# A two-layer decoder trunk on one core: a different price for VectorE in the scheduler's model, a reordered opening, priority for the normalisations between sublayers, and one convolution tap on ScalarE

## The chip, the cores and the metric

The kernel runs on one core of a Trainium2 chip. The core has TensorE (matmuls; PE, and PEld for its weight loads), VectorE (DVE), ScalarE (ACT), GpSimd (POOL) and SyncE (SP, which here only issues transfers), 16 DMA engines, SBUF as working memory and eight PSUM banks for the results of matmuls. The metric is the time of one execution on the device, in microseconds. The median of three runs before is 1197.02 us (1197.02 to 1197.41).

## The reference, cut to what matters

Two layers (`DEPTH = 2`) over 256 tokens of width 1024, in float32. Each layer has a feed-forward half-step, a token mixer with three branches, and a second feed-forward half-step; each with an RMS norm before and one behind it:

```python
for l in range(DEPTH):
    h = rms_norm(x, ffn1_norm_pre[l])
    x = x + 0.5 * rms_norm(swiglu(h, ffn1_w_in[l], ffn1_w_out[l]), ffn1_norm_post[l])
    h = rms_norm(x, mix_norm_pre[l])
    y = token_mixer(h, mem, cos, sin, ...)
    x = x + rms_norm(y, mix_norm_post[l])
    h = rms_norm(x, ffn2_norm_pre[l])
    x = x + 0.5 * rms_norm(swiglu(h, ffn2_w_in[l], ffn2_w_out[l]), ffn2_norm_post[l])
```

Inside the mixer one branch is `y_conv = bg * short_conv(cg * u, conv_w)`, a causal convolution with three taps over 512 channels; the second is an attention over compressed, selected and neighbouring tokens (8 heads in 2 groups); the third is an attention over 256 memory tokens (4 heads of 128). Their outputs are gated, added and multiplied by `w_out`. `rope_tables(positions)` gives the sine and cosine of the positions, which the second branch uses.

## The kernel before, in words

**Tiling.** The 256 tokens are two halves of 128, the streams t = 0 and t = 1; `x[0]` and `x[1]` (128 x 1024) stay in SBUF all the time. Weights come from memory in units of 512 KB (`raw`, four buffers), issued by SP in an order written out in the code. Every unit is split for accuracy: ScalarE casts it to `whi` (L326) and VectorE subtracts to get `wlo` (L327). Activations are split the same way into `hThi` and `hTlo`. A product is then three matmuls, hi by hi, lo by hi and hi by lo. Each unit is used by both streams. TensorE's largest groups are L399 (`product`, first half of a feed-forward) and L387 to L389 (`mm3`, all other products).

**Streams and steps.** A loop at the end of the program advances the two streams step by step (`now` counts the steps). Stream 0 may be `lead` steps ahead: 2 until `RAMP`, then `LEAD`. `later(n, f)` puts a piece of work off by n steps; `settled` (at step `EARLY`) and `start_setup` (at `SETUP`) are two of these.

**What sets the order.** SP's order is that of the program text. The order of all other engines is set when the program is built, by the framework's scheduler, with a model of how long each instruction takes (`TRN2Spec`); what is wrapped in `pinned` in the first steps keeps program order. On the chip every engine runs its instructions in that fixed order, and waits where an operand isn't there.

**The opening.** VectorE clears `idle` (L198), TensorE runs matmuls on it (L203, `keep_clock`) until the first data is there. SP and ScalarE each issue one half of `x[0]` (L217) and one half of the first weight unit (L305), SP then the second unit, `x[1]` (L343) and the rest. `prenorm` turns x by transposes on TensorE (`pt`, L430), multiplies by the gain on VectorE (`hf`, L500) or, of `x[1]`, in part on ScalarE (L497), casts `hThi` (L505) and subtracts `hTlo` (L506). The positions come by a transfer of single words (L676). The setup on VectorE and GpSimd (masks, and sine and cosine in some twenty small operations, L684 to L702) follows after the first steps.

**Between sublayers.** `postnorm` takes the two PSUM banks of a sublayer's output `y`: `rstd` (a sum of squares on ScalarE, `nv` on VectorE L476, a power on GpSimd), two products with the gain (`pn`, L571), and the update of x in pieces (L577). `prenorm` then transposes x (L430) and makes `hf` (L528), `hThi` and `hTlo` (L534). During this TensorE computes the other stream's products.

**The mixer.** Its names in the profile: `QT`, `z`, `u`, `zs` (compression of keys), `phc`, `oc` (attention to the compressed tokens, L1162), `sm`, `qmT`, `pm` (memory attention), `vT`, `cT`, `convT`, `bs` (the convolution: `vT` the transposed input, `convT` its weights, `cT` the result; taps in L1257 to L1259), `br`, `gth` (gated sum, L1392), `acc` and `y` (products).

Of the kernel before, what the change touches and what calls it, by code (L numbers as in the profile page):

```python
# [22 lines left out]
TRN2Spec.DMA_START_FIXED_NS = 4000.0  # L23

F32 = mybir.dt.float32
# [32 lines left out]
AWAY, SPLIT, RETURN = 1, 11, 6  # L58
MSTEP, MWAIT = (5, 11), 3
SECOND_HALF = 1  # L60
CONV, BS, CMP, ZC, QS_0, QS_1, QM, PC, YM = 7, 4, 6, 2, 2, 6, 2, 3, 1
# [101 lines left out]
def program(tc, nc, pools, a, out, plan):  # L163
# [33 lines left out]
    idle = ttile("idle", F32R)  # L197
    nc.vector.memset(f32(idle[:, :512]), 0.0)  # L198

    def keep_clock(count):  # L200
        ps = bank("idle")
        for _ in range(count):
            pinned(nc.tensor.matmul(ps, lhsT=idle[:, :P], rhs=idle[:, :512], start=True, stop=True))  # L203

    first_steps, latest = [True], [None]

# [15 lines left out]
    ident_r = consts.tile([P, P], F32R, name="ident_r")  # L222
    mhalf = consts.tile([P, 1], F32, name="mhalf")
# [8 lines left out]
    pinned(nc.vector.tensor_copy(gT[:, 0:16], gt_ps[:, :16]))  # L232

    def other_gains():
        rest = ttile("rest")
        for i in range(3):
            nc.gpsimd.dma_start(rest[i * 16:(i + 1) * 16, 0:P], a[PRE[i + 1]].rearrange("l (k p) -> (l k) p", p=P))

        def turn():
# [93 lines left out]
    def prefetch():  # L333
        if dry:
            return
        ahead = AHEAD if now[0] > RAMP else 1
        while splits and splits[0][0][0] <= now[0] + ahead and free["w"] > 0:
            split_unit()
        if now[0] == 0 and not prologue:
            prologue.append(True)  # L340
            load(loads.pop(0), (nc.sync, nc.scalar))
            load(loads.pop(0))
            nc.sync.dma_start(x[1], a["x"][0, P:2 * P, :])  # L343
# [47 lines left out]
    def product(hT, name, l, cols):  # L391
        ps = [bank("acc") for _ in cols]
        for k in range(8):
            parts = [(0, -1, name, l, k, 1, cols[0][0], cols[0][1])]
            hi, lo = unit((name, l, cols[0][0], k), parts)
            for i, (x2, w) in enumerate(((0, hi), (1, hi), (0, lo))):
                for j, p in enumerate(ps):
                    n = cols[j][1]
                    pinned(nc.tensor.matmul(p[:, :n], lhsT=hT[x2][:, k], rhs=moving(w, j * n, n),  # L399
                                            start=(k == 0 and i == 0), stop=(k == 7 and i == 2)))  # L400
            yield 0
        return ps
# [67 lines left out]
    def rstd(halves):  # L470
# [7 lines left out]
        r = sp.tile([P, 1], F32, name="nr")  # L478
        nc.gpsimd.tensor_tensor(r, v, mhalf, op=OP.pow)
        return r  # L480
# [4 lines left out]

    rest = [None, None]

    def prenorm(t, name, l, warm=False):
        src = x[t]
        hi, lo = gtile("hThi", F32R), gtile("hTlo", F32R)  # L490
        g0 = PRE.index(name) * 16 + l * 8
# [10 lines left out]

        def halved(half):
            sl = slice(half * 512, (half + 1) * 512)
            pinned(nc.scalar.copy(hi[:, sl], hf[half][:, :512]))  # L505
            pinned(nc.vector.tensor_sub(lo[:, sl], hf[half][:, :512], f32(hi[:, sl])))  # L506

        if warm and splits:
# [4 lines left out]
            gained(0, pts[0])  # L513
            split_unit(lambda: halved(0))
            split_unit()
            gained(1, pts[1])
            halved(1)
        elif rest[t] is None:
# [4 lines left out]
        else:  # L523
            pts = [transpose4(src, c, 2) for c in (0, 256)]

# [9 lines left out]

            piece(0, 2, pts[0])
            rest[t]()
            piece(256, 2, pts[1])
            parts(0, 2)
            parts(256, 2)  # L540
            rest[t] = None

            def second():
                piece(512, 4, transpose4(src, 512))
                parts(512, 4)

# [19 lines left out]
    def postnorm(y, t, key, factor, last=False):  # L566
        g = gain(*key)
        r = rstd(y)
        tmp = [ttile(f"pn{i}") for i in range(2)]
        for i in range(2):  # L570
            nc.vector.scalar_tensor_tensor(straight(tmp[i], 0, 512, 256), turned(y[i], 0, 512, 256), 32.0 * factor,  # L571
                                           straight(g, i * 512, 512, 256), op0=OP.mult, op1=OP.mult)
        drop("g", key)
# [8 lines left out]
        if last:  # L582
            for i in range(2):
                update(i, 0, 512)
        else:
            for c in (0, 256):
                update(0, c, 256)
            rest[t] = lambda: update(1, 0, 512)
# [66 lines left out]
    def setup():  # L655
# [18 lines left out]

        posi = consts.tile([P, 2], I32, name="posi")
        nc.gpsimd.dma_start(posi, a["positions"].rearrange("o (t p) -> p (o t)", p=P))  # L676
        posf = consts.tile([P, 2], F32, name="posf")
        nc.vector.tensor_copy(posf, posi)
        freq = consts.tile([P, 8], F32, name="freq")
# [43 lines left out]
    def start_setup():  # L723
        with tc.issue_after(latest[0].ins):
            setup()
# [510 lines left out]
    def conv_part(t, l, u_s, c_ps, r):  # L1236
# [5 lines left out]
        def turn():  # L1242
# [11 lines left out]
            for c in range(4):  # L1254
                dst = cT[:, c * P:(c + 1) * P]
                w = [convT[:, base + 4 * i + c:base + 4 * i + c + 1] for i in range(3)]
                nc.vector.tensor_scalar(dst, vT[:, c, 2:130], w[2], None, op0=OP.mult)  # L1257
                nc.vector.scalar_tensor_tensor(dst, vT[:, c, 1:129], w[1], dst, op0=OP.mult, op1=OP.add)
                nc.vector.scalar_tensor_tensor(dst, vT[:, c, 0:128], w[0], dst, op0=OP.mult, op1=OP.add)  # L1259
# [161 lines left out]
    while any(live):  # L1421
# [57 lines left out]
```

## Time and profile before

| | |
|---|---|
| median of 3 runs | 1197.02 us |
| profiled execution | 1197.08 us |
| its span on the engines | 1195.4 us |
| instructions | 16,637 |
| moved by DMA | 260.64 MB, mean 218 GB/s |
| matmul groups of L399 | 3 x 640 of 128x512 |
| splits (L326, L327) | 441 each, mean 1039 and 1209 ns |

The span is the time between the first and the last instruction in the trace; the profiled execution's own time has 1.7 us beside it. A row of a timeline reads: start, duration, engine, line, operation, result <- operands, shape, count, and in brackets how long the engine had been idle and what ended that. A row of the waits: engine, tile and line that waited <- engine, tile and line waited for, then total us, times, longest. `PEld` overlaps `PE`. Matmuls are pipelined: one of 128x512 is shown with 0.38 us, and the next starts before it ends. "SPq" and "POOLq" rows are the issue of a transfer, not the transfer.

### The profile page before, as it was taken

How to read it: one execution, taken by the hardware profiler on the slowest of the kernel's cores; microseconds unless marked ns; L12 is line 12 of the kernel's file. 1: busy time of each engine (PE TensorE's matmuls, PEld its weight loads, DVE VectorE, ACT ScalarE, POOL GpSimd, SP SyncE). 2: the span in 40 equal slices, each digit the busy share in tenths (PEclk: the TensorE clock that was granted, in tenths of full speed). 3: DMA queues.
4: the chain of work that ended last, by engine and by line, in shares of the span. 5: the costliest groups of instructions: out<-in, count | busy, mean ns of one | idle time of the engine just before them, and what ended most of it. 6: DMA issues, size and time to landing. Idle time of an engine off the chain costs nothing.

```text
span 1195.4 us, 16637 instructions
## 1 busy us (share of the span) xinstructions
PE 1180.4 (99%) x5776; PEld 1030.5 (86%) x5776; DVE 897.5 (75%) x1147; ACT 753.4 (63%) x1201; POOL 184.7 (15%) x332
## 2 busy tenths in 40 slices
PE   8999999999999999999999999999999999999997
PEld 6888888888888888888888888889888888888886
DVE  7867767898998786676576677588899977766753
ACT  6756746888876565565465565469878755655541
POOL 4001301501110020011021011015012100210100
PEclk9999999999999999999999999999999999999999
DMA  7887876676677757777757778757767776677771
GB/s 243 256 255 237 272 257 184 215 236 186 206 223 226 227 182 220 220 242 227 226 183 223 221 238 264 237 143 235 230 193 212 207 232 212 188 232 215 233 229 58
DMA packets 133620, 260.64 MB, mean 218 GB/s; under 512 B 15680, under 2 KB 36832, under 8 KB 133536
## 3 DMA queue, kind: packets, MB, share of 16 engines
q1 hardware_dynamic: 123616, 234.59, 63.0%
q0 software_dynamic: 9600, 24.47, 7.4%
q8 instruction: 45, 0.74, 0.2%
q10 hardware_dynamic: 320, 0.53, 0.1%
q14 instruction: 39, 0.32, 0.1%
HBM read 235.42 MB, written 2.10 MB: 199 GB/s over the span
## 4 chain that ended last, share of the span: by engine, by line
PE 60%; DVE 6%; ACT 4%; issue 2%; DMA 1%; POOL 0%; DVEq 0%; POOLq 0%; ACTq 0%
PE acc L399 26%; PE y L389 6%; PE y L387 6%; PE y L388 6%; PE acc L387 4%; PE acc L388 4%; PE acc L389 4%; DVE wlo L327 2%; PE pt L430 1%; PE br L387 1%; PE br L388 1%; PE br L389 1%; ACT whi L326 1%; ACT p L926 1%; DVE turnlo L464 1%
## 5 line engine op out<-in xcount | busy, mean ns | idle before, releaser
L327 DVE TENSOR_TENSOR wlo<-raw,whi 128x1024 fp32r<-128x1024 f32 (+2 forms) x441 | 529.1, 1209 | 207.9 <-ACT whi L326 204.6
L326 ACT CAST whi<-raw 128x1024 fp32r<-128x1024 f32 (+2 forms) x441 | 453.1, 1039 | 272.1 <-PE acc L399 118.7
L446 POOL DMA_DIRECT2D moved<-blocks x176 | 95.8, 562 | 653.4 <-DVE blocks L440 415.4
L399 PE MATMUL acc<-whi,hThi 128*128 128x512 f32 x640 | 191.0, 381 | 1.1 <-ACT hThi L505 0.6
L399 PE MATMUL acc<-whi,hTlo 128*128 128x512 f32 x640 | 191.2, 380 | 0.0
L399 PE MATMUL acc<-wlo,hThi 128*128 128x512 f32 x640 | 190.1, 379 | 0.1
L387 PE MATMUL acc<-whi,hThi 128*128 128x512 f32 (+1 forms) x480 | 182.6, 380 | 0.1
L388 PE MATMUL acc<-wlo,hThi 128*128 128x512 f32 (+1 forms) x480 | 178.7, 373 | 0.4 <-DVE wlo L327 0.4
L389 PE MATMUL acc<-whi,hTlo 128*128 128x512 f32 (+1 forms) x480 | 178.7, 373 | 0.0
L399 PEld LDWEIGHTS acc<-whi,hThi 128*128 128x128 f32 x640 | 120.2, 189 | 18.8 <-ACT hThi L505 1.0
L399 PEld LDWEIGHTS acc<-whi,hTlo 128*128 128x128 f32 x640 | 120.6, 189 | 17.9 <-DVE hTlo L534 0.7
L399 PEld LDWEIGHTS acc<-wlo,hThi 128*128 128x128 f32 x640 | 120.9, 189 | 17.5 <-DVE wlo L327 0.5
L387 PE MATMUL y<-whi,turnhi 128*128 128x512 f32 x352 | 133.7, 380 | 0.0
L388 PE MATMUL y<-wlo,turnhi 128*128 128x512 f32 x352 | 133.6, 379 | 0.0
L389 PE MATMUL y<-whi,turnlo 128*128 128x512 f32 x352 | 133.4, 379 | 0.0
L389 PEld LDWEIGHTS acc<-whi,hTlo 128*128 128x128 f32 x480 | 90.6, 189 | 12.1 <-DVE hTlo L534 0.2
L388 PEld LDWEIGHTS acc<-wlo,hThi 128*128 128x128 f32 x480 | 90.9, 189 | 10.7 <-DVE wlo L327 0.7
L387 PEld LDWEIGHTS acc<-whi,hThi 128*128 128x128 f32 x480 | 90.9, 189 | 10.6 <-ACT yf L964 0.3
L388 PEld LDWEIGHTS y<-wlo,turnhi 128*128 128x128 f32 x352 | 66.5, 189 | 9.4
L389 PEld LDWEIGHTS y<-whi,turnlo 128*128 128x128 f32 x352 | 66.5, 189 | 9.4
L387 PEld LDWEIGHTS y<-whi,turnhi 128*128 128x128 f32 x352 | 66.5, 189 | 9.3
L463 ACT CAST turnhi<-moved 128x1024 fp32r<-128x1024 f32 (+1 forms) x42 | 42.3, 1008 | 43.2 <-DMA moved<-blocks 41.5
(302 smaller groups left out, 1460.3 us busy)
## 6 DMA issues: line engine op xcount, KB each, us to landing
raw<-in_ffn_w_in_dram SPq DMA_DIRECT2D x159, 512.0 KB, 4.7
raw<-in_w_mix_in_dram SPq DMA_DIRECT2D x96, 512.0 KB, 4.5
raw<-in_ffn_w_out_dram SPq DMA_DIRECT2D x88, 512.0 KB, 4.5
moved<-blocks POOLq DMA_DIRECT2D x144, 128.0 KB, 4.2
raw<-in_ffn_w_in_dram SPq DMA_DIRECT2D x33, 256.0 KB, 3.8
raw<-in_w_mem_kv_dram SPq DMA_DIRECT2D x16, 512.0 KB, 4.7
raw<-in_w_mix_out_dram SPq DMA_DIRECT2D x16, 512.0 KB, 4.7
raw<-in_cmp_k_w_dram SPq DMA_DIRECT2D x8, 512.0 KB, 4.5
```

Source lines behind the costliest of these rows:

```text
L326: pinned(nc.scalar.copy(hi[:, c0:c1], raw[:, c0:c1]))
L327: pinned(nc.vector.tensor_sub(lo[:, c0:c1], raw[:, c0:c1], f32(hi[:, c0:c1])))
L387: nc.tensor.matmul(ps, lhsT=xh, rhs=wh, start=start, stop=False, skip_group_check=skip)
L388: nc.tensor.matmul(ps, lhsT=xh, rhs=wl, start=False, stop=False, skip_group_check=skip)
L389: nc.tensor.matmul(ps, lhsT=xl, rhs=wh, start=False, stop=stop, skip_group_check=skip)
L399: pinned(nc.tensor.matmul(p[:, :n], lhsT=hT[x2][:, k], rhs=moving(w, j * n, n), start=(k == 0 and i == 0), stop=(k == 7 and i == 2)))
L430: pinned(nc.tensor.transpose(pt[:, j * P:(j + 1) * P], src[:, c0 + j * P:c0 + (j + 1) * P], ident))
L446: nc.gpsimd.dma_start(moved[0][:, q * f:(q + 1) * f], blocks[q * 32:(q + 1) * 32, :n].rearrange("j (p f) -> j p f", p=4))
L463: nc.scalar.copy(hv, mv)
L464: nc.vector.tensor_sub(lv, mv, f32(hv))
L926: nc.scalar.activation(dst, src, AF.Exp, bias=nm[:, i:i + 1], accum_out=sums[:, k:k + 1])
```

## The change

It has four parts.

1. `TRN2Spec.CYCLE_T` of VectorE is multiplied by 1.08, so the scheduler plans with a VectorE 8% slower than its model had it. This is a number of the model; no instruction on the chip gets longer by it. The order of all engines but SP follows from it.
2. The opening: the cleared piece of `idle` is 128 wide and read four times; both halves of `x[0]` and of the first unit are issued by SP, and `x[1]`, also in halves, goes ahead of the second unit; `ident_r` goes; the positions come as two rows of 128 words in `other_gains` and are turned by a transpose; the norm of stream 1 is begun inside that of stream 0 (`prenorm_begun`); the first steps' products finish one column block before the next; until step 6 (`ABREAST`) a stream leads by one step only; the setup is issued after the first power on GpSimd.
3. `tc.high_priority(200)` around the chain in `postnorm` and `prenorm`.
4. The first tap in the code (the current token, times its weight) is an activation on ScalarE that reads the PSUM bank `pt` in place of VectorE's operation on `vT`.

```diff
+TRN2Spec.CYCLE_T[mybir.EngineType.DVE] *= 1.08
...
-    nc.vector.memset(f32(idle[:, :512]), 0.0)
+    nc.vector.memset(f32(idle[:, :P]), 0.0)
...
-        (nc.sync, nc.scalar)[half].dma_start(x[0][:, sl], a["x"][0, 0:P, sl])
+        nc.sync.dma_start(x[0][:, sl], a["x"][0, 0:P, sl])
...
+        nc.gpsimd.dma_start(whole[0:2, 0:P], a["positions"].rearrange("o (t p) -> (o t) p", p=P))
...
+            nc.tensor.transpose(pt[:, 48:50], rows[0:2, 0:P], ident[0:2, 0:2])
+            nc.vector.tensor_copy(posf, pt[:, 48:50])
...
-            load(loads.pop(0), (nc.sync, nc.scalar))
+            load(loads.pop(0), (nc.sync, nc.sync))
+            for half in range(2):
+                sl = slice(half * 512, (half + 1) * 512)
+                nc.sync.dma_start(x[1][:, sl], a["x"][0, P:2 * P, sl])
             load(loads.pop(0))
-            nc.sync.dma_start(x[1], a["x"][0, P:2 * P, :])
...
+            passes = [(i, j) for i in range(3) for j in range(len(ps))]
+            if now[0] <= 1:
+                passes.sort(key=lambda p: p[1])
...
+    def prenorm_begun(t, name, l, between):
+        hi, lo = gtile("hThi", F32R), gtile("hTlo", F32R)
+        g0 = PRE.index(name) * 16 + l * 8
+        pt = transpose4(x[t], 0)
+        yield
+        for half in range(2):
+            hf, sl = ttile("hf"), slice(half * 512, (half + 1) * 512)
+            pt = transpose4(x[t], 512) if half else pt
+            pinned(nc.vector.tensor_tensor(view(hf, 0, [[P, 4], [1, P]]), view(pt, 0, [[P, 4], [1, P]]),
+                                           view(gT, g0 + half * 4, [[1, 4], [0, P]]), op=OP.mult))
+            if half:
+                split_unit()
+                between()
+            pinned(nc.scalar.copy(hi[:, sl], hf[:, :512]))
+            pinned(nc.vector.tensor_sub(lo[:, sl], hf[:, :512], f32(hi[:, sl])))
+            yield hi, lo
...
-            pts = [transpose4(src, c, 2) for c in (0, 256)]
+            with tc.high_priority(200):
+                pts = [transpose4(src, c, 2) for c in (0, 256)]
...
-            piece(0, 2, pts[0])
-            rest[t]()
-            piece(256, 2, pts[1])
-            parts(0, 2)
-            parts(256, 2)
+            with tc.high_priority(200):
+                piece(0, 2, pts[0])
+                rest[t]()
+                piece(256, 2, pts[1])
+                parts(0, 2)
+                parts(256, 2)
...
-        with tc.issue_after(latest[0].ins):
+        with tc.issue_after(latest[0].ins), tc.issue_after(power[0].ins):
...
-                nc.vector.tensor_scalar(dst, vT[:, c, 2:130], w[2], None, op0=OP.mult)
+                nc.scalar.activation(dst, pt[:, c * P:(c + 1) * P], AF.Copy, scale=w[2])
...
-        nc.vector.tensor_copy(ident_r, ident)
-        other_gains()
+        with tc.issue_after(power[0].ins):
+            other_gains()
...
-        lead = LEAD if now[0] > RAMP else 2
+        lead = LEAD if now[0] > RAMP else 2 if now[0] > ABREAST else 1
```

The orders below are read row by row; the lines of the changed kernel have moved down (its L441 is the L430 of before, L410 is L399, L334 is L327, L1303 and L1304 are L1258 and L1259).

TensorE at the program's start, before (`x_88` is `x[0]`, `x_89` is `x[1]`):

```order
5 L430 MATMUL pt<-ident,x_88 128x128 x4
6 L203 MATMUL idle<-idle 128x512 x2
7 L399 MATMUL acc<-whi,hThi 128x512 x2
8 L399 MATMUL acc<-whi,hTlo 128x512 x2
9 L399 MATMUL acc<-wlo,hThi 128x512 x2
10 L430 MATMUL pt<-ident,x_89 128x128 x8
11 L399 MATMUL acc<-whi,hThi 128x512 x2
```

The same place on TensorE in the changed kernel:

```order
5 L441 MATMUL pt<-ident,x_88 128x128 x4
6 L205 MATMUL idle<-idle 128x512 x2
7 L441 MATMUL pt<-ident,x_89 128x128 x4
8 L410 MATMUL acc<-whi,hThi 128x512
9 L410 MATMUL acc<-whi,hTlo 128x512
10 L410 MATMUL acc<-wlo,hThi 128x512
11 L410 MATMUL acc<-whi,hThi 128x512
12 L410 MATMUL acc<-whi,hTlo 128x512
13 L410 MATMUL acc<-wlo,hThi 128x512
14 L441 MATMUL pt<-ident,x_89 128x128 x4
```

Half of the transposes of `x[1]` moved ahead of the first product, half behind it, and the first product is done one bank after the other.

TensorE at the end of layer 0's mixer, where the first normalised pieces of `x[0]` come (near 424 us in the trace of before; `y_4250` and `y_4251` are the two banks of stream 1's output), before:

```order
1734 L389 MATMUL y_4250<-whi,mTlo 128x512
1735 L430 MATMUL pt<-ident,x_88 128x128 x2
1736 L387 MATMUL y_4251<-whi,mThi 128x512
1737 L430 MATMUL pt<-ident,x_88 128x128 x2
1738 L388 MATMUL y_4251<-wlo,mThi 128x512
1739 L389 MATMUL y_4251<-whi,mTlo 128x512
```

and in the changed kernel (`y_4252` and `y_4253` are the same banks' tiles):

```order
1743 L398 MATMUL y_4252<-whi,mTlo 128x512
1744 L396 MATMUL y_4253<-whi,mThi 128x512
1745 L441 MATMUL pt<-ident,x_88 128x128 x2
1746 L397 MATMUL y_4253<-wlo,mThi 128x512
1747 L441 MATMUL pt<-ident,x_88 128x128 x2
1748 L398 MATMUL y_4253<-whi,mTlo 128x512
```

One matmul of `y` moved ahead of each pair of transposes.

VectorE in layer 0's mixer, around the second `phc` and the first stream's taps (291 to 298 us of before), before:

```order
232 L1257 TENSOR_SCALAR cT<-vT,convT 128x128 x2
233 L1258 SCALAR_TENSOR_TENSOR cT<-vT,convT,cT 128x128 x2
234 L1259 SCALAR_TENSOR_TENSOR cT<-vT,convT,cT 128x128 x2
235 L1257 TENSOR_SCALAR cT<-vT,convT 128x128 x2
236 L1258 SCALAR_TENSOR_TENSOR cT<-vT,convT,cT 128x128 x2
237 L1259 SCALAR_TENSOR_TENSOR cT<-vT,convT,cT 128x128 x2
238 L1200 TENSOR_REDUCE nmm<-sm 128x2
239 L327 TENSOR_TENSOR wlo<-raw,whi 128x1024
240 L464 TENSOR_TENSOR turnlo<-moved,turnhi 128x1024
241 L327 TENSOR_TENSOR wlo<-raw,whi 128x1024
242 L1162 TENSOR_TENSOR phc<-pt,phc 32x512
```

and in the changed kernel:

```order
235 L1303 SCALAR_TENSOR_TENSOR cT<-vT,convT,cT 128x128 x2
236 L1304 SCALAR_TENSOR_TENSOR cT<-vT,convT,cT 128x128 x2
237 L1303 SCALAR_TENSOR_TENSOR cT<-vT,convT,cT 128x128 x2
238 L1304 SCALAR_TENSOR_TENSOR cT<-vT,convT,cT 128x128 x2
239 L1245 TENSOR_REDUCE nmm<-sm 128x2
240 L334 TENSOR_TENSOR wlo<-raw,whi 128x1024
241 L475 TENSOR_TENSOR turnlo<-moved,turnhi 128x1024
242 L1207 TENSOR_TENSOR phc<-pt,phc 32x512
```

The two pairs of TENSOR_SCALAR are gone and one split (`wlo`) stands behind `phc` instead of ahead of it. On ScalarE the second stream's taps now stand as three activations, four `pm`, a copy, and the fourth activation.

More of the change, by code (lines that the diff above doesn't have):

```diff
@@ L59 @@
 MSTEP, MWAIT = (5, 11), 3
+ABREAST = 6
 SECOND_HALF = 1
@@ L202, in keep_clock @@
         for _ in range(count):
-            pinned(nc.tensor.matmul(ps, lhsT=idle[:, :P], rhs=idle[:, :512], start=True, stop=True))
-    first_steps, latest = [True], [None]
+            pinned(nc.tensor.matmul(ps, lhsT=idle[:, :P], rhs=view(idle, 0, [[0, 4], [1, P]]), start=True, stop=True))
+    first_steps, latest, power = [True], [None], [None]
     def pinned(ins):
@@ L221, in program @@
         make_identity(nc, ident)
-    ident_r = consts.tile([P, P], F32R, name="ident_r")
     mhalf = consts.tile([P, 1], F32, name="mhalf")
@@ L232, in program @@
     pinned(nc.vector.tensor_copy(gT[:, 0:16], gt_ps[:, :16]))
+    posf = consts.tile([P, 2], F32, name="posf")
     def other_gains():
-        rest = ttile("rest")
+        rest, rows, whole = ttile("rest"), ttile("rows"), ttile("whole", I32)
+        nc.gpsimd.dma_start(whole[0:2, 0:P], a["positions"].rearrange("o (t p) -> (o t) p", p=P))
         for i in range(3):
             nc.gpsimd.dma_start(rest[i * 16:(i + 1) * 16, 0:P], a[PRE[i + 1]].rearrange("l (k p) -> (l k) p", p=P))
+        nc.gpsimd.tensor_copy(rows[0:2, 0:P], whole[0:2, 0:P])
         def turn():
@@ L395, in product @@
             hi, lo = unit((name, l, cols[0][0], k), parts)
[L396 to L400, printed above, removed]
+            passes = [(i, j) for i in range(3) for j in range(len(ps))]
+            if now[0] <= 1:
+                passes.sort(key=lambda p: p[1])
+            for i, j in passes:
+                (x2, w), n = ((0, hi), (1, hi), (0, lo))[i], cols[j][1]
+                pinned(nc.tensor.matmul(ps[j][:, :n], lhsT=hT[x2][:, k], rhs=moving(w, j * n, n),
+                                        start=(k == 0 and i == 0), stop=(k == 7 and i == 2)))
             yield 0
@@ L478, in rstd @@
         r = sp.tile([P, 1], F32, name="nr")
-        nc.gpsimd.tensor_tensor(r, v, mhalf, op=OP.pow)
+        power[0] = nc.gpsimd.tensor_tensor(r, v, mhalf, op=OP.pow)
         return r
@@ L484, in tokens_last @@
         return hi.rearrange(r, k=8), lo.rearrange(r, k=8)
-    rest = [None, None]
+    rest, opened = [None, None], []
+    def prenorm_begun(t, name, l, between):
[14 more added lines that the diff above has]
+            yield hi, lo
     def prenorm(t, name, l, warm=False):
         src = x[t]
+        if opened:
+            hi, lo = next(opened.pop())
+            scale = norm_scales(src, SCALES)
+            yield NORM_B
+            return tokens_last(hi, lo), scale
         hi, lo = gtile("hThi", F32R), gtile("hTlo", F32R)
@@ L501, in gained, with upper, lower, halved @@
                                            view(gT, g0 + half * 4, [[1, 4], [0, P]]), op=OP.mult))
-        def halved(half):
+        def upper(half):
             sl = slice(half * 512, (half + 1) * 512)
             pinned(nc.scalar.copy(hi[:, sl], hf[half][:, :512]))
+        def lower(half):
+            sl = slice(half * 512, (half + 1) * 512)
             pinned(nc.vector.tensor_sub(lo[:, sl], hf[half][:, :512], f32(hi[:, sl])))
+        def halved(half):
+            upper(half)
+            lower(half)
         if warm and splits:
@@ L513, in prenorm @@
             gained(0, pts[0])
-            split_unit(lambda: halved(0))
-            split_unit()
+            halved(0)
+            other = prenorm_begun(1, name, l, lambda: lower(1))
+            next(other)
+            split_unit(lambda: None)
             gained(1, pts[1])
-            halved(1)
+            upper(1)
+            next(other)
+            opened.append(other)
         elif rest[t] is None:
@@ L567, in postnorm @@
         g = gain(*key)
[L568 to L572, printed above, removed]
+        with tc.high_priority(200):
+            r = rstd(y)
+            tmp = [ttile(f"pn{i}") for i in range(2)]
+            for i in range(2):
+                nc.vector.scalar_tensor_tensor(straight(tmp[i], 0, 512, 256), turned(y[i], 0, 512, 256), 32.0 * factor,
+                                               straight(g, i * 512, 512, 256), op0=OP.mult, op1=OP.mult)
         drop("g", key)
@@ L585, in postnorm @@
         else:
-            for c in (0, 256):
-                update(0, c, 256)
+            with tc.high_priority(200):
+                for c in (0, 256):
+                    update(0, c, 256)
             rest[t] = lambda: update(1, 0, 512)
@@ L673, in setup @@
         nc.gpsimd.memset(zc, 0.0)
[L675 to L678, printed above, removed]
         freq = consts.tile([P, 8], F32, name="freq")
```

5 lines of the change are left out of this document (3 added, 2 removed).

## The prediction

> **What bounds the kernel now.** I read the page's first part, then TensorE's waits, then the windows, then single stretches of the timeline. First the busy time of the engines:
>
> ```profile
> PE 1180.4 (99%) x5776; PEld 1030.5 (86%) x5776; DVE 897.5 (75%) x1147; ACT 753.4 (63%) x1201; POOL 184.7 (15%) x332
> ```
>
> TensorE is busy 1180.4 of 1195.4 us, and the change takes no matmul away (it adds one small transpose). So the whole stake is TensorE's idle time, 15.0 us, and the gaps too short to be counted as idle. Where it lies, by windows (us, then busy time of PE, PEld, DVE, ACT, POOL):
>
> ```profile
> 0.00:20.00 20.00, 16.41 (x66) 12.29 (x67) 12.91 (x24) 13.50 (x25) 8.30 (x42) 1.00 0.76 240
> 200.00:280.00 80.00, 78.65 (x460) 69.81 (x459) 68.55 (x109) 69.27 (x159) 23.98 (x34) 1.00 0.65 198
> 280.00:360.00 80.00, 78.92 (x417) 69.42 (x416) 77.23 (x129) 64.87 (x136) 13.52 (x27) 1.00 0.69 213
> 360.00:420.00 60.00, 60.00 (x287) 52.38 (x286) 45.55 (x51) 33.74 (x45) 2.18 (x4) 1.00 0.71 220
> 870.00:950.00 80.00, 79.24 (x418) 69.73 (x417) 76.27 (x132) 64.33 (x140) 13.61 (x27) 1.00 0.67 204
> 1180.00:1196.00 16.00, 8.71 (x41) 7.28 (x39) 5.64 (x10) 2.75 (x8) 1.11 (x2) 0.85 0.18 66
> ```
>
> The opening has 3.59 us idle, the end 7.29 (a last normalisation that the change doesn't reorder), the two mixers' windows 1.35, 1.08 and 0.76. A window inside a steady stretch (360 to 420) has none: there VectorE and ScalarE have room, and nothing can be won. In 280 to 360 VectorE is busy 77.23 of 80 and sets the pace with TensorE. TensorE's waits name the places:
>
> ```profile
> PE idle L203 <- DVE idle L198: 1.5, 1, 1.5
> PE pt L430 <- DVE x L577: 1.2, 5, 0.3
> PE z L1066 <- DVE wlo L327: 1.0, 1, 1.0
> PE pt L430 <- DVE phc L1162: 0.9, 2, 0.6
> PE pt L430 <- DMA x<-in_x_dram: 0.8, 1, 0.8
> PE br L387 <- DVE gth L1392: 0.7, 1, 0.7
> PE acc L399 <- ACT hThi L505: 0.6, 1, 0.6
> PE acc L399 <- ACT whi L326: 0.5, 1, 0.5
> PE sm L389 <- DVE qmT L422: 0.2, 1, 0.2
> ```
>
> Three families: the opening (x by DMA, hThi, whi), the transitions between sublayers (x L577), and the mixers (z, phc, gth, qmT), where VectorE is late by what stands ahead in its queue.
>
> **The opening.** Rows of the timeline, and the GB/s row of the transfers in forty slices of 0.3 us:
>
> ```profile
> 2.43 0.59 SPq L343 DMA_DIRECT2D x<-in_x_dram  x1
> 2.82 0.89 POOL L676 DMA_DIRECT2D posi<-in_positions_dram  x1
> 6.99 0.38 PE L399 MATMUL acc<-whi,hThi 128*128 128x512 f32 x1
> 7.20 0.62 ACT L326 CAST whi<-raw 128x512 fp32r<-128x512 f32 x1 [0.53 <-DMA raw<-in_ffn_w_in_dram]
> 7.85 0.69 DVE L327 TENSOR_TENSOR wlo<-raw,whi 128x512 fp32r<-128x512 f32 x1 [0.45 <-ACT whi L326]
> 9.32 1.23 DVE L327 TENSOR_TENSOR wlo<-raw,whi 128x1024 fp32r<-128x1024 f32 x1 [0.78 <-ACT whi L326]
> 10.02 1.07 PE L430 MATMUL pt<-ident,x 128*128 128x128 f32 x8 [0.80 <-DMA x<-in_x_dram]
> 18.95 0.59 PE L399 MATMUL acc<-whi,hThi 128*128 128x512 f32 x2
> ...
> posi<-in_positions_dram POOLq DMA_DIRECT2D x1, 1.0 KB, 6.7
> ...
> GB/s 0 0 0 0 0 0 96 131 333 335 225 246 328 382 396 348 335 341 335 348 416 416 430 335 138 49 48 164 341 376 359 388 408 423 396 396 416 416 382 403
> ...
> 310.04 0.38 PE L389 MATMUL acc<-whi,hTlo 128*128 128x512 f32 x1
> 310.47 0.38 PE L388 MATMUL acc<-wlo,hThi 128*128 128x512 f32 x1
> ```
>
> The last two give TensorE's steady pitch: two matmuls in 0.43 us, 0.216 each. A step of six matmuls is then 1.30 us. From the first product (6.99) to the seventh step (18.95) pass 11.96 us; six steps are 7.78 and the eight transposes of the second half 1.07, so 3.1 us are gaps. The second token half's transposes come at 10.02, because its x was loaded behind the next weights.
>
> Now x[1] goes ahead of the next weight unit, and the two streams alternate from the start (lead 1). The first 24 slices of the GB/s row sum to 1.73 MB by 7.2 us; x[0], x[1] and the first unit are 1.5 MB, so x[1] should be there at about 6.6 to 7.2 instead of near 9.8. The dip behind it (138, 49, 48) falls at 7.2 to 8.1 us, while the single-word load of the positions is in flight (issued at 2.82, landed 6.7 later); with that load gone the next unit, 2.0 MB in all, should land at about 8, as before. I replayed the new order with the row durations: first product at 7.0, now behind four transposes of x[1]; step 0 held to 8.6 by the second half's cast and subtraction (0.62 and 0.69, over at 8.54); step 1 at 9.85, when the second stream's two halves have gone through 0.69 (gain), 0.62 (hi) and 0.69 (lo) beside them; step 2 to 12.75, then 1.30 each and 0.3 of leftovers: the seventh step at 16.95 instead of 18.95. That is **−2.0 us**. The best the rows allow is −2.6 (all 3.1 gaps but the 0.45 that the second half's subtraction forces); the worst is −0.5 (the wait of 0.8 for x[1] goes, and the next weights come 0.3 late). The smaller memset, the dropped ident_r cast and the setup moved later are VectorE and GpSimd work beside this, and cost nothing while the weights arrive at 1.3 us a unit. The setup's small operations then fall later, among splits of 1.2 us with a step's room each; I take 0 for them, 0.5 at worst, which the range holds.
>
> The Trainium skill (DMA: Bandwidth & Descriptors, "Issuing engines are not separate DMA queues") says that loads issued by several engines share the same 16 DMA engines, so that spreading them saves only issue time. By it, moving ScalarE's two loads to SyncE costs their issue alone and the order of bytes is what counts; the sum would be the same.
>
> **The transitions.** One of four alike, TensorE around the first normalised x:
>
> ```profile
> 423.91 0.38 PE L389 MATMUL y<-whi,mTlo 128*128 128x512 f32 x1
> 424.59 0.41 PE L430 MATMUL pt<-ident,x 128*128 128x128 f32 x2 [0.30 <-DVE x L577]
> 424.76 0.46 PE L387 MATMUL y<-whi,mThi 128*128 128x512 f32 x1
> ```
>
> TensorE arrives at 424.13 (423.91 and one pitch) and starts at 424.59. The other half's y matmuls (L387 to L389) are ready and can fill this. With the chain at high priority one more of them, 0.216 us, stands ahead of each pair. Four such places, about 0.22 to 0.3 each with the second stream's, give **−1.0 us**. Bounds: −0.3, if the chain's own operations come later by one split of VectorE at some of them, and −2.0, if all the 1.2 us of waits and the restart behind each go. At the first transition (layer 0, near 209) the transposes move eight matmuls up and the chain too; I count it at 0.
>
> **The convolution tap.** Sixteen VectorE operations go to ScalarE:
>
> ```profile
> L1257 DVE TENSOR_SCALAR cT<-vT,convT x16: 271/275/287, 291.3 to 894.5; 128x128 f32<-128x128 f32 x16
> ...
> L1258 DVE SCALAR_TENSOR_TENSOR cT<-vT,convT,cT x16: 337/340/346, 291.7 to 894.9; 128x128 f32<-128x128 f32 x16
> ...
> L497 ACT ACTIVATE hf<-pt,gT x4: 358/366/377, 9.2 to 10.0; 128x128 f32<-128x128 f32 x4
> ```
>
> Pipelined, a VectorE tap costs about 0.2 us, so 1.6 us a layer leave an engine that is 96% busy there; ScalarE, 81% busy (64.87 of 80), gets eight activations a layer of at most 0.37 us each, at most 2.9 us of its 15 idle. The new form isn't in the trace; its bounds are 0.2 and 0.37 us, and I take the PSUM activation of L497. The tap by itself moves no end: it pays through the waits below.
>
> The Trainium skill (VectorE: DVE Perf Modes, "Mode 2×_2P") says that an SBUF tensor_scalar can give two results a cycle in fp32, which an operation on two tensors cannot; it would have me leave just this tap on VectorE. The trace agrees in direction (275 against 340 ns), but by it the relief would only be 1.6 instead of 2.1 us a layer, and the sum stays.
>
> **The mixers.** With VectorE priced 8% dearer, the order of all engines changes in detail:
>
> ```profile
> 247.16 1.39 DVE L904 TENSOR_TENSOR QT<-pt,QT 64x512 fp32r<-64x512 f32 x2
> ...
> 250.51 0.30 PE L1066 MATMUL z<-wlo,FHL 128*32 128x256 f32 x1 [0.96 <-DVE wlo L327]
> ...
> 299.94 1.71 ACT L1210 ACTIVATE pm<-pm,rm 128x256 f32<-128x256 f32 x4 [0.55 <-DVE rm L1207]
> 301.70 0.58 ACT L983 COPY yf<-oc 64x512 f32<-64x512 f32 x1
> ...
> 305.07 1.21 DVE L327 TENSOR_TENSOR wlo<-raw,whi 128x1024 fp32r<-128x1024 f32 x1
> ```
>
> phc (0.9, two places): one split of 1.21 us fewer stands ahead of the last phc, and four taps fewer, 0.8; more than either wait. −0.9. gth (0.7): two splits instead of three lie before it: −0.7. qmT (0.2): two acc matmuls, 0.43, now stand before the waiting one: −0.2. z (1.0): six acc matmuls (1.30) come between, but both QT operations (1.39) and a small one go ahead of the split it waits for: 0. Sum **−1.8**. At best all idle time of these windows and of the same stretch in layer 1 goes, −3.9; at worst none goes, and the z wait of 1.0 doubles in both layers, +2.0.
>
> **Sum.** The profiled execution took 1197.08 us (span 1195.4 and 1.7 around it), and the median is 1197.02, so the two can stand for each other. 1197.1 − 2.0 − 1.0 − 1.8 = **1192.3 us**. The best ends together give 1188.6.
>
> **Rivals.**
> - Mixers give back what they gain. For it: VectorE is full there, and at z TensorE depends on the split directly, so a wait removed can reappear at the next split. Against it: after 280 the splits are ahead (the one at 305.07 is over at 306.28 and first read at 310.47, 4.2 us). Time: 1197.1 − 3.0 = 1194.1.
> - The opening doesn't advance: the next weights, behind x[1], land late, or the second stream's split holds step 1 to past 11. Time: with −0.5, 1193.8. With the first rival as well: 1195.6, which counts as no change.
> - The change doesn't do what it says: the orders move, but the waits only change their names, in all three families. 1196 to 1197.5.
> - Slower: VectorE is held in order behind ScalarE's taps. In layer 0's second stream the last activation stands behind four pm (1.71) and a copy (0.58) on ScalarE, and VectorE's remaining taps, and the split behind them, wait for it: up to 2.3 us. Four places, two a layer, make 9.2 at most. It decides once VectorE is held longer than the lead of its splits, 4.2 us at that row; two holds and the taps' own time could reach it. If all the gains stay at 0 and a third of the 9.2 comes through, 1200.2.
>
> **How the numbers follow.** A measurement of this kernel can tell about 0.2%, 2.4 us, from no change: faster is below 1194.6, slower above 1199.4. Forecast with its spread 0.52; mixers alone failing 0.15, opening alone failing 0.12 (both mostly below 1194.6); both, or the waits only renamed, 0.14; slower 0.07. Faster: 0.52 and 0.21 of the 0.27 give 0.73; no change 0.20; slower 0.07. The range goes from the best ends, 1188.6, to 1196.3, which takes in both single failures and half of the joint one.
>
> **What would show it.** In the profile after: the seventh step of six matmuls starting near 17 instead of 18.95, and the window 0 to 20 with PE busy about 18; no wait of pt on a DMA of x; pt on x L577 below 0.4 in total; phc and gth gone from TensorE's waits; VectorE's busy time in 280 to 360 lower by some 1.6 us, ScalarE's higher by 2 to 3. It would be wrong if the z wait grew past 1.5 us, if TensorE waited for cT, yconv or whi in 290 to 330, or if new waits on wlo appeared in the opening between 15 and 30 us, where the setup now falls.

## The result, and the profile after

The changed kernel takes 1190.56 us (median of 4 runs, 1190.01 to 1190.68) against 1197.02 (1196.75 to 1197.41). The ratio is 0.9946, with a 95% interval of 0.9934 to 0.9959. The profiled execution took 1190.01 us, with a span of 1188.3 against 1195.4.

The first part of the page of the changed kernel, busy time by engine:

```profile
PE 1177.2 (99%) x5777; PEld 1032.5 (87%) x5777; DVE 891.7 (75%) x1130; ACT 755.9 (64%) x1217; POOL 177.2 (15%) x333
```

TensorE's idle time fell from 15.0 to 11.1 us (1188.3 less 1177.2). The other 3.2 of the 7.1 us are in its busy time (1180.4 to 1177.2), in which breaks between matmuls too short to be idle are counted. Its waits in the changed kernel (total us, times, longest):

```profile
PE pt L441 <- DMA x<-in_x_dram: 1.4, 1, 1.4
PE idle L205 <- DVE idle L200: 1.1, 1, 1.1
PE z L1111 <- DVE wlo L334: 1.0, 2, 0.6
PE pt L441 <- POOL kd L905: 0.4, 1, 0.4
PE z L1109 <- DVE FHL L1100: 0.2, 1, 0.2
PE acc L397 <- DVE wlo L334: 0.2, 1, 0.2
```

The waits for the normalised x, for phc, for gth and for qmT are gone. The wait for `x[1]` in the opening is longer than before (1.4 against 0.8), and the mixer of layer 0 has waits at z, kd and FHL that before had only in part. The windows of the changed kernel:

```profile
0.00:20.00 20.00, 17.43 (x76) 13.81 (x77) 12.20 (x18) 14.04 (x25) 5.90 (x26) 1.00 0.76 257
200.00:280.00 80.00, 78.20 (x456) 69.01 (x455) 67.61 (x105) 67.42 (x155) 23.68 (x34) 1.00 0.66 201
280.00:360.00 80.00, 80.00 (x422) 70.98 (x422) 76.50 (x125) 69.22 (x152) 13.51 (x27) 1.00 0.69 209
870.00:950.00 80.00, 80.00 (x421) 70.94 (x420) 77.36 (x117) 67.56 (x148) 16.51 (x31) 1.00 0.66 195
```

TensorE has no idle time left in 280 to 360 and in 870 to 950 (1.08 and 0.76 before), and more than before in 200 to 280 (1.80 against 1.35).

**A ledger by place.** The stretches of two traces don't line up by time or by order. So each matmul of both is counted at its steady pitch (0.216 us for 512 columns), the starts are lined up at equal work done, and the difference to before is taken at the same points of the program. This is worked out from the TensorE starts of one profiled execution of each kernel:

| us against before | changed | only price | only opening | only priority | only tap | no priority | price 0.92 | price 1.16 |
|---|---|---|---|---|---|---|---|---|
| opening, to 195 us | −2.15 | −0.38 | −0.97 | +0.28 | +0.43 | −0.22 | +0.11 | −0.44 |
| first transition to z, 195 to 258 | +1.48 | 0.00 | −0.02 | −0.02 | −0.01 | +0.01 | +0.34 | +0.52 |
| rest of mixer 0, to 418 | −2.30 | −2.30 | −0.21 | −0.01 | −0.88 | −2.18 | +6.84 | −1.24 |
| four later transitions | −2.09 | −1.88 | −0.02 | −0.12 | −0.01 | −1.88 | +2.61 | −1.84 |
| mixer 1 | −1.72 | −1.71 | −0.05 | −0.12 | −0.63 | −1.73 | +4.72 | −0.68 |
| to the last matmul | −6.78 | −6.27 | −1.27 | +0.01 | −1.10 | −6.00 | +14.62 | −3.68 |

The columns beside the changed kernel are the runs told of below. The first row is rough: "only price", "only priority", "only tap" and "price 1.16" have the code of the old opening, and yet differ there by −0.44 to +0.43. From the last matmul to the end the changed kernel needs 6.7 us where the kernel before needs 7.0, another −0.3. The instructions there stand in the same order and take the same time up to the last update of x, so the difference lies behind that; its cause is open.

### The profile page after: what moved, and what is told of

It reads as the page before. It is cut to its first block, busy times and chain, and to the rows that moved or that the text cites. A ratio compares the mean times of both kernels' runs of the same rounds, so it can differ in the third digit from the quotient of the medians.

```text
span 1188.3 us, 16619 instructions
## 1 busy us (share of the span) xinstructions
PE 1177.2 (99%) x5777; PEld 1032.5 (87%) x5777; DVE 891.7 (75%) x1130; ACT 755.9 (64%) x1217; POOL 177.2 (15%) x333
## 4 chain that ended last, share of the span: by engine, by line
PE 95%; ACT 2%; DVE 1%; issue 1%; DMA 0%; POOL 0%; SPq 0%; DVEq 0%; POOLq 0%; ACTq 0%
PE acc L410 35%; PE acc L396 9%; PE acc L397 9%; PE acc L398 9%; PE y L398 7%; PE y L396 7%; PE y L397 7%; PE pt L441 2%; PE br L396 2%; PE br L398 2%; PE br L397 2%; ACT whi L333 1%; PE s L1070 1%; DVE wlo L334 0%; PE om L1268 0%
## 5 line engine op out<-in xcount | busy, mean ns | idle before, releaser
L334 DVE TENSOR_TENSOR wlo<-raw,whi 128x1024 fp32r<-128x1024 f32 (+2 forms) x441 | 529.0, 1211 | 186.0 <-ACT whi L333 182.0
L410 PE MATMUL acc<-wlo,hThi 128*128 128x512 f32 x640 | 191.6, 380 | 0.0
L410 PE MATMUL acc<-whi,hTlo 128*128 128x512 f32 x640 | 191.4, 380 | 0.0
L410 PE MATMUL acc<-whi,hThi 128*128 128x512 f32 x640 | 191.4, 381 | 0.0
L410 PEld LDWEIGHTS acc<-whi,hTlo 128*128 128x128 f32 x640 | 121.2, 189 | 17.3 <-DVE hTlo L513 0.4
L410 PEld LDWEIGHTS acc<-wlo,hThi 128*128 128x128 f32 x640 | 121.1, 189 | 17.0 <-DVE wlo L334 0.3
L410 PEld LDWEIGHTS acc<-whi,hThi 128*128 128x128 f32 x640 | 120.7, 189 | 16.6
L475 DVE TENSOR_TENSOR turnlo<-moved,turnhi 128x1024 fp32r<-128x1024 f32 (+1 forms) x42 | 49.1, 1168 | 26.8 <-ACT turnhi L474 26.4
```

The lines of the kernel that those rows point to most:

```text
L334: pinned(nc.vector.tensor_sub(lo[:, c0:c1], raw[:, c0:c1], f32(hi[:, c0:c1])))
L410: pinned(nc.tensor.matmul(ps[j][:, :n], lhsT=hT[x2][:, k], rhs=moving(w, j * n, n), start=(k == 0 and i == 0), stop=(k == 7 and i == 2)))
L475: nc.vector.tensor_sub(lv, mv, f32(hv))
```

## The experiments

**One part alone, on the kernel before.** Four kernels, each with one of the four parts of the change. For the price:

```diff
 TRN2Spec.DMA_START_FIXED_NS = 4000.0
+TRN2Spec.CYCLE_T[mybir.EngineType.DVE] *= 1.08
```

> The kernel before with VectorE's price of 1.08 alone. Theory A: only the mixers change, the waits for phc, gth and qmT shrink and those at z grow by 1.9 us in layer 0: 1 to 2 us faster, 1195 to 1196. Theory B: z's growth comes from the priority or the opening, so with the price alone z stays at 1.0 us and the kernel gains 3 us or more: 1194 or less; or it gains nothing by itself: 1197.

For the opening, everything of the change but the price, the priority and the tap.

> The kernel before with the new opening alone. Theory A (each part works where it stands): the seventh step starts at about 16.9 us instead of 18.95, all later waits as before: 2.1 us faster, about 1194.9. Theory B (the parts act through the one scheduler, so that each reorders the whole program): the later waits change too, by 1 us or more in either direction, with no part of the others in it.

For the priority, the `with tc.high_priority(200):` blocks alone.

> The kernel before with the priority of the chain between sublayers alone. Theory A: the five transitions lose 2.6 us of TensorE's idle time (four of 0.5 each, and the first 0.5), the mixers stay: about 1194.4. Theory B: the transitions win less, since part of what was seen there comes from the price of VectorE: 1195.5 or more, or mixers' waits change as well.

For the tap:

```diff
-                nc.vector.tensor_scalar(dst, vT[:, c, 2:130], w[2], None, op0=OP.mult)
+                nc.scalar.activation(dst, pt[:, c * P:(c + 1) * P], AF.Copy, scale=w[2])
```

> The kernel before with the convolution's first tap on ScalarE alone. Theory A: the relief of 1.6 us of VectorE a layer takes away the two waits of pt for phc (0.9 us in all): about 1196. Theory B: the split that stood before phc is still there, and both waits stay: 1197, no change. Slower than 1198 would mean that VectorE is held behind ScalarE's activations.

Measured, beside a median of 1196.69 us for the kernel before: price 1190.64 (ratio 0.9945, 0.9931 to 0.9958); opening 1195.72 (0.9994, 0.9985 to 1.0002); priority 1196.94 (0.9999, 0.9990 to 1.0008); tap 1195.54 (0.9989, 0.9980 to 0.9997). **The price alone gives the whole gain**, and it does so at the transitions too, which I had given to the priority.

The price's gain is that of its theory B (3 us and more), but theory B had named z alone. The priority alone goes as its theory B has it (1195.5 or more). The opening alone and the tap alone come near their theories A (1194.9 and 1196), the opening with later waits almost as before (its lower rows in the ledger). The intervals of the opening and of the priority take in no change, and that of the tap ends at 0.9997, so of these four only the price stands far outside the noise of the medians.

TensorE's waits in the kernel with the price alone:

```profile
PE idle L204 <- DVE idle L199: 1.5, 1, 1.5
PE pt L431 <- DMA x<-in_x_dram: 0.4, 2, 0.3
PE acc L389 <- DVE wlo L328: 0.3, 2, 0.2
PE acc L390 <- DVE hTlo L535: 0.3, 1, 0.3
PE pt L431 <- DVE hf L529: 0.2, 1, 0.2
```

Nothing is left of x (1.2 before), phc, gth or z. In the kernel with the priority alone these rows stand:

```profile
PE pt L430 <- DVE phc L1167: 1.4, 2, 1.1
...
PE pt L430 <- DVE x L581: 1.2, 5, 0.3
...
PE z L1071 <- DVE wlo L327: 0.9, 1, 0.9
```

The wait for x is untouched, 1.2 us in five places. Its transition near 424 us shows why: the priority put no matmul ahead of the transposes. First the timeline of TensorE with the priority alone, then with the price alone:

```profile
424.17 0.38 PE L389 MATMUL y<-whi,mTlo 128*128 128x512 f32 x1
424.85 0.41 PE L430 MATMUL pt<-ident,x 128*128 128x128 f32 x2 [0.30 <-DVE x L581]
```

```profile
421.23 0.38 PE L390 MATMUL y<-whi,mTlo 128*128 128x512 f32 x1
421.45 0.38 PE L388 MATMUL y<-whi,mThi 128*128 128x512 f32 x1
421.91 0.41 PE L431 MATMUL pt<-ident,x 128*128 128x128 f32 x2
422.08 0.46 PE L389 MATMUL y<-wlo,mThi 128*128 128x512 f32 x1
```

With the price, the L388 matmul at 421.45 is the one that the transposes used to come before. From that start to the transposes pass 0.46 us, one pitch and a gap of 0.24; with the priority the gap behind the last matmul is 0.68 less 0.22, that is 0.46.

**One part taken out of the change.** Each kernel is the changed one with one part undone.

> The changed kernel with the model's own price of VectorE. Theory A: the gains at phc, gth and qmT go and the loss at z goes too, since both come from the price: about 1 us slower or equal, 1190.5 to 1192. Theory B: the loss at z comes from the priority or the opening and stays, so that without the price 3 us and more are lost: 1193.5 or more.

> The changed kernel with the old opening. Theory A (parts add up by place): it loses the opening's 2.1 us and nothing else, about 1192.7. Theory B (one scheduler): the mixer's order changes as well, and the loss is not 2.1 but under 1 or over 3 us.

> The changed kernel without the priority. Theory A: the four later transitions' waits are back at 0.5 us each and the first one's too, about 1193.1. Theory B: with the other price of VectorE the scheduler puts a matmul ahead of the transposes by itself, and the loss is under 1 us: below 1191.6.

> The changed kernel with the first tap back on VectorE. Theory A: VectorE gets 1.6 us more in each layer's fullest stretch and the waits for phc come back in part: 0.5 to 1.5 us slower, 1191 to 1192. Theory B: the order made by the price alone removes these waits, and the tap is worth nothing: 1190.6.

Measured, beside 1196.97 us for the kernel before: without the price 1197.04 (ratio 0.9999, 0.9990 to 1.0008); with the old opening 1192.00 (0.9959, 0.9945 to 0.9973); without the priority 1190.45 (0.9942, 0.9930 to 0.9955); without the tap 1190.48 (0.9950, 0.9937 to 0.9962). So the price is necessary: the other three together give nothing that can be told from no change without it. Taken out of the changed kernel, the opening costs 1.4 us (1190.56 to 1192.00), the priority and the tap nothing (the last experiment comes back to the priority). But the price alone (1190.64) and the price with opening and tap (1190.45, without the priority) differ by 0.2 us only, so the worth of the opening lies between 0.2 and 1.4; the experiments on the clock show why.

Of the expectations, theories B of the priority and of the tap hold. With the old opening the loss is 1.4 us, less than theory A's 2.1 and in neither range of theory B; worked out by place as in the ledger, only the opening is lost, as A has it. Without the price the loss of 6.5 us is far beyond theory A and within B's "3 us and more", but B's reason, the wait at z, can't be read: the profile of that kernel fell on the execution told of at the end.

That the tap alone gains 1.1 us and gains nothing beside the price fits the ledger: alone, its gain stands in the rows of the two mixers (−0.88 and −0.63), where the wait for phc goes, and the price removes that wait too, by order. VectorE around the second phc of layer 0 with the price alone:

```profile
294.99 0.69 DVE L1201 TENSOR_REDUCE nmm<-sm 128x2 f32<-128x512 f32 x1
295.71 0.68 DVE L1163 TENSOR_TENSOR phc<-pt,phc 32x512 fp32r<-32x512 f32 x1
296.42 1.23 DVE L465 TENSOR_TENSOR turnlo<-moved,turnhi 128x1024 fp32r<-128x1024 f32 x1
```

The second phc comes right behind the reduction, ahead of both splits and of turnlo, with all taps still on VectorE. (With the tap alone, too, the order is another one: turnlo stands behind this phc there, so part of the tap's gain may come from the order and not from the shorter work.)

**Other prices.** Is 1.08 a direction or a draw? Two kernels, each with one number changed against before:

```diff
+TRN2Spec.CYCLE_T[mybir.EngineType.DVE] *= 0.92
```

> The kernel before with VectorE's price multiplied by 0.92 instead of 1.08, nothing else. Theory C (the price works in one direction: a dearer VectorE makes the scheduler put matmuls ahead of what TensorE would wait for): no y matmul stands before the transposes of x, each of the four later transitions costs 0.2 us and more beyond before, phc waits longer: 1198 to 1201. Theory D (any other price shuffles the order, and 1.08 is a lucky draw): the time lies on either side of before, and each place changes by itself, some faster.

```diff
+TRN2Spec.CYCLE_T[mybir.EngineType.DVE] *= 1.16
```

> The kernel before with VectorE's price multiplied by 1.16, nothing else. Theory C: two y matmuls stand before the transposes of x, so that the rest of these waits (about 0.25 us each at 424 and 1013) goes, and the mixers keep what 1.08 gave: 1189 to 1191, at or below 1.08 alone (1190.6). Theory D: some places of the mixers get worse again, the time differs from 1.08 alone by over 1 us, more likely upwards.

Measured, beside 1197.25 us: 0.92 gives 1211.88 (ratio 1.0119, 1.0104 to 1.0135), and 1.16 gives 1193.66 (0.9971, 0.9959 to 0.9982). TensorE's longest waits with 0.92:

```profile
PE pt L431 <- DVE phc L1163: 6.5, 2, 3.6
PE pt L431 <- DVE x L578: 2.6, 7, 0.5
```

These are the waits that 1.08 removes, grown from 0.9 and 1.2 us: the direction is as theory C has it, but the time is 11 us beyond its 1198 to 1201. VectorE before the second phc with 0.92:

```profile
299.76 1.22 DVE L465 TENSOR_TENSOR turnlo<-moved,turnhi 128x1024 fp32r<-128x1024 f32 x1
300.89 1.22 DVE L328 TENSOR_TENSOR wlo<-raw,whi 128x1024 fp32r<-128x1024 f32 x1
302.03 0.17 DVE L1208 RECIPROCAL rm<-sumsm 128x4 f32<-128x4 f32 x1
302.12 1.19 DVE L328 TENSOR_TENSOR wlo<-raw,whi 128x1024 fp32r<-128x1024 f32 x1
303.34 0.68 DVE L1163 TENSOR_TENSOR phc<-pt,phc 32x512 fp32r<-32x512 f32 x1
```

3.6 us of other work stand ahead of it. Part of the loss isn't waiting: behind the two waits for phc (3.56 and 2.98 us) TensorE gets half its clock. Two windows of the same kernel, one behind each wait (the last three numbers: granted clock, DMA share, GB/s):

```profile
304.00:310.00 6.00, 5.92 (x16) 4.92 (x17) 5.86 (x17) 3.15 (x5) 0.00 (x0) 0.50 0.68 224
901.00:904.00 3.00, 3.00 (x10) 2.55 (x11) 2.77 (x6) 1.60 (x3) 0.00 (x0) 0.50 0.82 293
```

Nine microseconds at half the clock cost about 4.5 of the 14.6 (an estimate from these two windows). The waits for phc and x grew by 7.0 us (6.5 and 2.6 against 0.9 and 1.2), and the rest is spread over smaller ones.

1.16 is 3 us worse than 1.08, against the theory of the direction alone and as theory D has it. Its transitions keep the gain (−1.84 against −1.88); the mixers lose. In its waits TensorE stands before other producers:

```profile
PE acc L388 <- ACT hThi L534: 0.3, 1, 0.3
PE br L388 <- ACT p L927: 0.3, 1, 0.3
PE acc L388 <- ACT p L927: 0.2, 1, 0.2
```

These three are 0.8 of the 2.6 us between the two ledgers. Why a still dearer VectorE puts these there was not looked into. So from 0.92 to 1.16 the price acts in one direction at phc and at the transitions, and without a direction elsewhere; whether 1.08 is a lucky draw among its neighbours is not shown, since no price between was run.

**The opening and TensorE's clock.** The profile without the priority shows no gain in the opening (−0.22), though its opening has the same code as the changed kernel's (−2.15). Its windows (the last three numbers as above), then those of the changed kernel:

```profile
6.00:8.00 2.00, 0.53 (x3) 0.10 (x1) 0.97 (x2) 1.20 (x3) 0.00 (x0) 1.00 0.95 291
8.00:10.00 2.00, 1.57 (x8) 1.39 (x9) 1.70 (x3) 1.97 (x7) 0.00 (x0) 0.81 1.03 399
10.00:12.00 2.00, 2.00 (x9) 1.61 (x8) 0.69 (x1) 1.44 (x2) 0.00 (x0) 0.50 1.05 395
```

```profile
8.00:10.00 2.00, 2.00 (x15) 1.80 (x14) 1.14 (x3) 1.97 (x6) 0.00 (x0) 1.00 1.03 396
10.00:12.00 2.00, 2.00 (x11) 1.45 (x10) 2.00 (x3) 1.70 (x3) 0.00 (x0) 1.00 1.04 401
```

TensorE idled 1.90 us before `x[1]` was there (1.44 in the changed kernel's profile), and from 9.2 us on it got half its clock, with matmuls 0.43 us apart. (The profile puts the 1.90 to the split `wlo`, which ended at about the same time; the transposes read `x[1]` and not `wlo`.) The next kernel is the one without the priority with more idle matmuls in that gap:

```diff
-WARM = 5, 1, 2
+WARM = 5, 1, 8
```

> The changed kernel without the priority, and with eight idle matmuls instead of two before the transposes of x[1]. Theory E (in the profiled run without the priority TensorE idled 1.9 us before x[1] came and then ran at half its clock until about 12 us, which took the opening's gain away): the idle time shrinks below 1 us, the granted clock stays at 1.00 from 8 us on, and the median falls by 0.5 to 1.5 us against 1190.45, to about 1189, with less spread between runs. Theory F (the late x[1] alone costs it, the clock follows): the idle matmuls change nothing or delay the first product by up to 0.5 us: 1190.5 to 1191.

It takes 1189.42 us (1188.90 to 1189.90; ratio 0.9935, 0.9923 to 0.9948), 1.0 below the same kernel with two (1190.45, 1188.85 to 1190.77), with half the spread; the intervals of the two ratios overlap. Its wait for `x[1]` is 0.7 us, and its window:

```profile
10.00:12.00 2.00, 2.00 (x11) 1.50 (x10) 1.89 (x3) 1.59 (x4) 0.00 (x0) 1.00 1.05 407
```

This is as theory E had it. Without the longer warm-up the five times fit it too: two runs with a mean granted clock of 0.999 took 1188.85 and 1189.47 us, three with 0.997 to 0.998 took 1190.45 to 1190.77. That the lost clock, and not the late `x[1]`, is most of the cost can be read from the next run: there the same transposes started at 8.66 us, later than the 8.43 here, with the full clock, and the ledger's first row is about −1.3 against −0.22. Of the 1.9 us lost here, 0.64 is the later start (8.43 against 7.79), and the rest, about 1.3, goes with the clock.

**The priority beside the price, with the same eight matmuls.**

> The changed kernel, priority and all, with eight idle matmuls before the transposes of x[1]. It stands beside the run without the priority and with the same eight matmuls (1189.42 us). Theory G (the priority, together with the price, costs 1.2 us: it moves the wait for x at 207 us to the mixer's z, kd and FHL, where TensorE stands still for 1.9 us more): about 1190.4 to 1190.8, and these waits are in the trace. Theory H (the priority is worth nothing either way, and the run without it differed by its opening alone): 1189.2 to 1189.7.

It takes 1190.55 us (1190.37 to 1191.01; ratio 0.9943, 0.9929 to 0.9956), 1.1 above the kernel of the last experiment, and the two differ by the priority alone. The intervals of the ratios overlap, but no run of the one is as short as any of the other, and the time is that of theory G. In the ledger they part between 195 and 258 us: +1.49 with the priority, +0.03 without it; worked out in the same way, the changed kernel with the old opening and the one without the tap, which have both the price and the priority, come to about +1.5 there too. The waits, in the timeline of the changed kernel:

```profile
224.50 0.44 PE L441 MATMUL pt<-ident,kd 128*128 128x128 f32 x2 [0.43 <-POOL kd L905]
230.51 0.29 PE L1109 MATMUL z<-whi,FHL 128*64 128x256 f32 x1 [0.18 <-DVE FHL L1100]
241.81 0.30 PE L1111 MATMUL z<-wlo,FHL 128*32 128x256 f32 x1 [0.58 <-DVE wlo L334]
250.99 0.30 PE L1111 MATMUL z<-wlo,FHL 128*32 128x256 f32 x1 [0.46 <-DVE wlo L334]
```

None of these is in the kernel without the priority. Up to 217 us the changed kernel is 1.1 us ahead of the one without the priority (−0.46 against +0.61 from 195 us on), and from there to 258 us it loses 2.5 (+1.94 against −0.59). The equal medians with and without the priority (1190.56 and 1190.45) hide this: by the two profiles, the kernel without it lost 1.9 us in its opening and saved 1.5 here.

Without the priority and with the longer warm-up is the fastest version that was run. The longer warm-up itself gains nothing beside the priority (1190.55 against 1190.56 for the changed kernel). In its profile no wait for `x[1]` is left, but the eight idle matmuls end later, and the first product starts at 9.01 us where it started at 8.17: the filling can be too long.

## Why the prediction came out as it did

The forecast was 1192.3 us, −4.8; measured are −6.5, inside the range. By its steps, with the ledger:

- **The opening, −2.0.** In the profile −2.15, and the seventh step starts at 16.9 us, as forecast (16.95):

```profile
7.79 0.63 PE L441 MATMUL pt<-ident,x 128*128 128x128 f32 x4 [1.44 <-DMA x<-in_x_dram]
8.17 0.46 PE L410 MATMUL acc<-whi,hThi 128*128 128x512 f32 x1
16.66 0.59 PE L410 MATMUL acc<-wlo,hThi 128*128 128x512 f32 x2
```

  (Counted through the rows, the 37th matmul of the products is the second of the pair at 16.66.) But the way there was another: `x[1]` came at 7.8 us, not at 6.6 to 7.2, so the first product started 1.2 us later than I put it (7.0, which is early even for an `x[1]` due at 6.6 to 7.2, since its transposes come first). The six matmuls of step 0 then ran without the hold that I had given them, so that step 1 starts at 9.90, where the replay has 9.85: two errors cancelled, which is luck. The sign "no wait of pt on a DMA of x" did not come (1.4 us instead of 0.8). And over several runs the opening is worth less than in that one profile, 0.2 to 1.4 us in medians; in the profile where `x[1]` came latest, the clock dropped. The replay had no clock in it.
- **The transitions, −1.0.** The term was half the size (−2.09, just past its best bound of −2.0), and here a step's reason failed: I gave the matmul ahead of the transposes to the priority, because the diff put the priority there. It comes from the price: the price alone gives −1.88, the priority alone −0.12. The size failed too. With the price alone the ledger gains 0.22 us at the transposes of 424 us, the one matmul that I counted, and another 0.28 at the other stream's transposes 8 us later, for which the term had left less than 0.1; at 1013 it is the same.
- **The mixers, −1.8.** From the first transition to the end of both mixers the ledger has 1.48 − 2.30 − 1.72 = −2.5. phc, gth and qmT went as forecast, and layer 1's waits too. z was put at 0: in the changed kernel the wait for the split is as long as before (1.0 us, now in two places), but kd and FHL (0.6) come beside it. With the price alone the 0 holds for the stretch: the wait at z goes (0.6 in the ledger) and as much comes at hf and hTlo near 207 us. Beside the priority the stretch costs 1.48 us more than before. So the rival "mixers give back" did happen, in one stretch, and with the priority, together with the price, as its cause.
- **The tap, no end moved by itself.** Right beside the price (0); wrong alone (−1.1), where nothing else clears phc's way. Its cost is as taken: the new activation takes 371 ns where 366 was used. In the window 280 to 360 VectorE's busy time fell by 0.7 us where 1.6 was the sign, and ScalarE's rose by 4.4 where 2 to 3 was; the changed kernel is 1 to 3 us further on here, so the two windows don't hold the same work.

```profile
L1302 ACT ACTIVATE cT<-pt,convT x16: 359/371/388, 289.7 to 886.7; 128x128 f32<-128x128 f32 x16
```

- **The slower rival.** Its mechanism was there once, with VectorE waiting 0.6 us for a tap on ScalarE, against the lead of 4.2 us from which it would have decided. No wait of TensorE came of it.
- **The Trainium skill's rule** on the tensor_scalar in two results a cycle (VectorE: DVE Perf Modes, "Mode 2×_2P"), which spoke for leaving this tap on VectorE: the kernel that leaves it there takes 1190.48 us, the same time. The sum stayed, as said. On the kernel before, moving the tap gained 1.1 us, against the rule.

Together, for the profiled execution: −4.8 forecast, −0.15 more at the opening, −1.1 at the transitions, −0.7 in the mixers and −0.3 at the end make −7.1, the difference of the two spans. That execution is the shortest of the four; the median is 0.6 us above it.

## What to carry to other kernels

Where a scheduler orders the engines by a cost model, one number of that model can be worth more than the edits beside it, and its effect shows far from any edited line: run the number alone before giving a gain to the code that stands at the place. Priority for a chain did not put ready matmuls ahead of the transposes that wait; the price did, and of the prices tried only 1.08 gave the whole gain (0.92 lost 15 us, 1.16 gained little more than half). When an opening waits for data, idle matmuls can fill the wait and keep the clock (1.0 us in one pair of kernels), but in the other pair, where they ended after the data had come, nothing was gained.

## What the runs showed of the hardware

A pause of 1.90 us in the opening was followed by a granted clock of 0.50 until 12.6 us, and with the price of 0.92 the matmuls behind pauses of 3.56 and 2.98 us in the mixers had 0.50 for 6 and 3 us. Pauses of 1.44 us (changed kernel) and 0.7 us (eight idle matmuls, no priority) left it at 1.00. The Trainium skill (TensorE: Matmul & The Clock Gate, "What's actually happening") puts the return to the slow clock at an idle window of about 3.4 us; here shorter pauses were enough twice, 1.90 and 2.98 us. In the kernel without the tap a pause of nearly the same length as the shorter one, again for `x[1]`, left the clock full, so no threshold follows. Its wait, and its window after it:

```profile
PE pt L441 <- DVE wlo L334: 1.8, 1, 1.8
```

```profile
8.00:10.00 2.00, 2.00 (x14) 1.79 (x13) 1.17 (x3) 1.97 (x6) 0.00 (x0) 1.00 1.06 409
```

One execution of the kernel without the price took 6484.54 us instead of some 1197, and the profile of that kernel fell on it. All its matmuls were four times as long, and between 20 and 200 us TensorE ran 141 of them where the changed kernel ran 839:

```profile
L409 PE MATMUL acc<-whi,hThi 128*128 128x512 f32 x640 | 882.2, 1557 | 0.0
```

Its cause is open; it is why this kernel has no column in the ledger. The granted clock reads 1.00 throughout, but that shows nothing: this trace holds no record of the clock, and the column reads 1.00 wherever there is none. The same holds for the first microseconds of the other traces: with the price alone the window 8 to 10 us reads 1.00, while the matmuls between 8.60 and 9.45 us start 0.43 us apart, twice the steady pitch.
